# Projection weights squared and halved three tiles after their loads, sparse keys and queries loaded one tile ahead, in a hybrid attention step

## The chip, the cores and the metric

The kernel runs on one core of a Trainium2 chip. The core's engines work side by side, each through its own list of instructions in order: PE (TensorE, matrix products), DVE (VectorE), ACT (ScalarE), POOL (GpSimd), and SP (SyncE), which here only issues transfers. ACT and POOL can issue transfers too; a transfer is then an entry in that engine's list. An instruction waits at the head of its engine until what it reads has been written and what it overwrites has been read, and all that stands behind it on the engine waits with it. The metric is the time of one execution on the device in microseconds (us).

## The reference

One step of a layer with two kinds of attention on a prompt of 1024 tokens and on 8 sequences of 8 new tokens (the samples), each with 512 cached ones. The width is 1024, a head has 64 columns.

```python
h = rms_norm(x, g_norm)
proj = einsum('btd,dn->btn', h, w_in)      # w_in: 1024 x 3872, split into q, k, v, gates of both kinds
# NSA: 8 query heads, 2 key/value heads; compressed blocks, selected blocks, a window of 512
o_a = g0 * attend(q, kc, vc) + g1 * attend(q, k_selected, v_selected) + g2 * attend(q, k_window, v_window)
# FoX: 8 heads, softmax(q k / 8 + sum of log forget gates), causal
o_b = fox(q, k, v, cumsum(log f))
y = x + concat(o_a * silu(z_a), o_b * silu(z_b)) @ w_out
```

Keys and queries are normalised per head (QK-norm), those of NSA turned by rotary angles. The outputs are y for prompt and samples and the new keys and values of every cache.

## The kernel before

**The projection in chunks.** The columns of w_in are worked off in 15 chunks, of 256 columns each but one of 288: cmp, slc, win, qa twice, kb twice, qb twice, vb twice, z four times. For each chunk there are nine tiles: eight of 128 prompt tokens and one of the 64 sample tokens. PE cannot take the wide floats at full rate, so x and the weights are each halved into a high and a low part of 16 bits. A prompt tile is 24 products (eight slices of the width, three products each, the line of `acc<-wsp,xth` and `acc<-wsp,xtl`, L246); a sample tile is 16 (`acc<-wsp,xts`, L239). The weights change from chunk to chunk, so all nine tiles of a chunk read the chunk's halves, wsp.

**Loading and halving weights.** `load_w` gets a chunk's weights ready in four quarters: quarter q is loaded into a buffer wst (L198, on SP, four buffers in all), squared on ACT with a running sum by row (vsq, L202, the sums in the columns of vst). A product with ones on PE (tr, L205) adds the rows up; DVE (L206, L207) and POOL (a power, L208) make a scale of it. Then each quarter is scaled and split: ACT writes the high half (L216 and L217, or L220 alone), DVE (L221) or POOL (L218) the low one, both into wsp, of which there are eight, for two chunks. Called at tile 1 of a chunk, `load_w` is written for the next chunk. The first product of the next chunk cannot start before its first quarter is split.

**Background.** While the chunks run, other work is traced in between at tile 3 of a chunk: the compression of cached keys (cpair is loaded, turned on PE into ctr at L467, copied by ACT into cx or cy at L469 and multiplied, sa, L475), masks, gates, and `wout_squares`, which loads two slices of w_out each time (xin) and squares them on ACT (xsq, L813) for the scale of w_out.

**What sets the order.** The program is traced in one order; a scheduler then orders each engine's list with a simulation of its own, in which a transfer takes a time that need not be the chip's. It moves an instruction ahead when that simulation has it ready. `tc.keep_in_program_order` holds an instruction behind the one that was traced just before it on its engine.

**FoX and the start of NSA.** After eleven chunks FoX attention runs, with the z chunks as filler: PE makes scores st, ACT exponentials pf (L716) and their high half phi (L719), PE multiplies with the values (pv). Near its end `nsa_first` starts the sparse attention, then `nsa_tile` runs eight tiles of 128 queries. For a tile t, `nsa_keys(t)` loads the tile's selected and window keys (kn, two transfers, L1056 and L1057) and `nsa_queries(t)` the queries (nq, L1069), from outputs and from scratch in DRAM. `split16` scales them on ACT in place (L1049), rounds to the high half (L1050) and subtracts on POOL. PE turns them, ACT copies them (k1a, nq) and issues a transfer within the core to the masked operands kma (L1065) and nqm (L1081). `nsa_tile(t)` calls both for tile t + 1 at its start. PE's scores for the maximum (smax, L1103) read kma and nqm.

Of the kernel before, what the change touches and what calls it, by code (L numbers as in the profile page):

```python
# [21 lines left out]
D = 1024  # L22
NT = 8
# [70 lines left out]
def layer_kernel(ctx, tc, a, o):  # L94
# [84 lines left out]
    bank = {"tr": ("ctr", 1), "acc": ("acc", 4, 288), "ws": 2}  # L179
    w_in = a["w_in"][0].rearrange("(kt p) n -> p kt n", p=128)  # L180

    def load_w(cols, vcols=None, vi=None, split=None):

        n = sum(c1 - c0 for c0, c1 in cols)
        sv = W.tile([128, 24], F32, name="vst", bufs=3)
# [8 lines left out]
        for q in range(4):  # L194
            s = W.tile([128, 2, 288], F32, name="wst", bufs=4)
            i = 0
            for c0, c1 in cols:
                nc.sync.dma_start(s[:, :, i:i + c1 - c0], w_in[:, 2 * q:2 * q + 2, c0:c1])  # L198
                i += c1 - c0
            sq = W.tile([128, 2, 288], F16, name="vsq", bufs=1)  # L200
            for c, x in spans:
                nc.scalar.activation(sq[:, :, c], s[:, :, c], AF.Square, accum_out=sv[:, x + q:x + q + 1])  # L202
            st.append(s)
        p = PS.tile([128, 12], F32, name="tr", bufs=bank["ws"])
        nc.tensor.matmul(p[:, 0:used], ones, sv[:, 0:used], start=True, stop=True)  # L205
        nc.vector.tensor_reduce(out=sv[:, 12:13], in_=p[:, 0:used], axis=AX.X, op=ALU.add)  # L206
# [20 lines left out]
        if vcols is not None:  # L227
# [3 lines left out]
            nc.gpsimd.tensor_tensor(vsc[:, vi, 0:1], sv[:, 17:18], nhalf[:, 0:1], op=ALU.pow)  # L231
            nc.vector.reciprocal(vsc[:, vi, 1:2], vsc[:, vi, 0:1])
            nc.vector.tensor_tensor(un[:, 3:4], vsc[:, vi, 0:1], un[:, 0:1], op=ALU.mult)
        return parts, n, un

    def sample_product(ps, x, w):
        for k in range(KT):
# [566 lines left out]

    w_out = a["w_out"][0].rearrange("(kt p) n -> p kt n", p=128)

    def wout_squares(ks):

        for k in ks:
            s = B.tile([128, D], F32, name="xin", bufs=5)  # L810
            tc.keep_in_program_order(nc.sync.dma_start(s, w_out[:, k]))
            junk = B.tile([128, D], F32, name="xsq")
            nc.scalar.activation(junk, s, AF.Square, accum_out=wsc[:, k:k + 1])  # L813

    def wout_scale():

# [9 lines left out]
    def wout_split(pool, k):  # L826
# [4 lines left out]
        for h in range(2):  # L831
# [11 lines left out]
    chunks += [("z", [(1304, 1560)], 0), ("z", [(1560, 1816)], 1), ("z", [(3360, 3616)], 2), ("z", [(3616, 3872)], 3)]  # L843
    tabs = {"cmp": None, "slc": 1, "win": 2, "qa": 0}
    background = {1: [cmp_weights, cmp_prompt_tokens], 2: [lambda: cmp_cached(0)], 3: [lambda: cmp_cached(1)],
                  4: [lambda: cmp_cached(2)], 5: [lambda: cmp_cached(3), lambda: wout_squares((0, 1))],
                  6: [sample_compressed, lambda: score_scales(), lambda: wout_squares((2, 3))],
                  7: [setup_masks, finish_gates, lambda: wout_squares((4, 5))],
                  8: [fox_decay, load_logf, lambda: wout_squares((6, 7))], 9: [fox_first, wout_scale]}

    def score_scales():

# [24 lines left out]
    def load_chunk(ci):  # L877
        kind, cols, c = chunks[ci]
        vi = {"slc": 0, "win": 1, "vb": 2 + c}.get(kind)
        return load_w(cols, None if vi is None else slice(128, 256) if vi < 2 else slice(0, 256), vi,  # L880
                      True if kind == "z" else None)

    def project_chunk(ci, tab, wn):
        kind, cols, c = chunks[ci]
# [64 lines left out]
    first_loads()  # L949
    x_tile(0)  # L950
    setup()
    loaded = load_chunk(0)
    x_tile(1)
    nc.sync.dma_start(rope, a["c_rope"])
    for ci in range(11):
        if ci == 9:
            vb16 = C.tile([128, NT, 8, 130], F16, name="vb16", tag="vb16")
            nc.vector.memset(vb16[:, :, :, 64:65], 1.0)
        w = loaded
        for t in project_chunk(ci, tab, w):  # L960
            if t == 1:
                loaded = load_chunk(ci + 1)
            if t == 3:
                for f in background.get(ci, ()):
                    f()
    S1.close()


# [13 lines left out]
    def rest():  # L982
        w = loaded
        for ci in range(11, 15):
            n = None
            for t in project_chunk(ci, tab, w):
                if t == 1 and ci < 14:
                    n = load_chunk(ci + 1)
                yield t
            w = n  # L990

    filler = rest()
    quota = [0.0]
# [54 lines left out]
    def split16(src, s, hi, lo, e=nc.gpsimd):  # L1048
        nc.scalar.activation(src, src, AF.Copy, scale=s)  # L1049
        nc.scalar.activation(hi, src, AF.Copy)  # L1050
        e.tensor_sub(lo, src, hi)

    def nsa_keys(t):
        ks = BN.tile([128, 4, 128], F16, name="nks", bufs=1)
        kn = BN.tile([128, 4, 64], F32, name="kn")
        nc.sync.dma_start(flat(kn[:, 0:2]), outs["slc"][0][t * 128:(t + 1) * 128, 0:128])  # L1056
        nc.sync.dma_start(flat(kn[:, 2:4]), p_win[(t - 4) * 128:(t - 3) * 128, 0:128] if t >= 4 else kpark[t])  # L1057
        split16(kn, nsc[:, 0:1], ks[:, :, 0:64], ks[:, :, 64:128], nc.gpsimd if t else nc.vector)
        p = turned(t)
        for i in range(4):  # L1060
            nc.tensor.transpose(p[:, i * 128:(i + 1) * 128], ks[:, i], ident16)
        pk = p.rearrange("p (i n) -> p i n", i=4)
        c = slice(t * 128, (t + 1) * 128)
        nc.scalar.activation(k1a[:, :, c], pk, AF.Copy)
        nc.scalar.dma_start(kma[0:64, :, c], k1a[0:64, :, c])  # L1065

    def nsa_queries(t):
        q = BN.tile([128, 8, 64], F32, name="nq", bufs=1)
        nc.sync.dma_start(q.rearrange("p h d -> p (h d)"), qpark[t])  # L1069
        qsp = BN.tile([128, 8, 128], F16, name="nqs", bufs=1)  # L1070
        split16(q, nsc[:, 1:2], qsp[:, :, 64:128], qsp[:, :, 0:64], nc.gpsimd if t else nc.vector)
        r = []
        for g in range(2):
            p = turned(t)
            for i in range(4):
                nc.tensor.transpose(p[:, i * 128:(i + 1) * 128], qsp[:, 4 * g + i], ident16)
            q1 = BN.tile([128, 512], F16, name="nq1", bufs=4)
            qm = BN.tile([128, 512], F16, name="nqm", bufs=4)
            nc.gpsimd.memset(qm[64:88], 0.0)
            nc.scalar.activation(q1, p, AF.Copy)  # L1080
            nc.scalar.dma_start(qm[0:64], q1[64:128])  # L1081
            r.append((q1, qm))
        return r
# [104 lines left out]

    def nsa_first():

        nc.gpsimd.memset(kmc, 0.0)
        nc.gpsimd.memset(k1c, 0.0)
        nc.gpsimd.dma_start(kma[64:88].rearrange("p k n -> p (k n)"), a["c_kind"][:, 0:4 * T])
        for g in range(2):
            nc.gpsimd.dma_start(kmc[64:88, g, 64 * g:64 * g + 64], a["c_kind"][:, 4 * T:4 * T + 64])
        nc.gpsimd.dma_start(stair, a["c_stair"])
        nsa_keys(0)
        qq = nsa_queries(0)
        csp = BN.tile([64, 2, 128], F16, name="csp", bufs=1)
        nc.vector.memset(csp, 0.0)  # L1200
        split16(ck_p, nsc[0:63, 0:1], csp[0:63, :, 0:64], csp[0:63, :, 64:128])
        p = turned(0)
        for g in range(2):
# [220 lines left out]
    units = [(b, f, g) for b in range(NB) for f, g in ((sample_nsa, sample_nsa_out), (sample_fox, sample_fox_out))]  # L1424
    units.append((None, None, None))

    def nsa_tile(t, qq):
        qn = None
        if t + 1 < NT:
            nsa_keys(t + 1)  # L1430
            qn = nsa_queries(t + 1)
        oa = B3.tile([128, 8, 64], F32, name="oa", bufs=6)
        if t:
            nsa_max(1, t, qq[1][1])
# [22 lines left out]
    fox_early(7)  # L1457
    for g in range(2):
        nsa_max(g, 0, qq[g][1])
    fox_attend(7, 1)  # L1460
    SC.close()
    BE = B3 = S3.enter_context(tc.tile_pool(name="nsl", bufs=1, reuse_waits="tile"))
# [14 lines left out]
    mixed[0] = 1  # L1477
    for t in range(4):
        load_wout(2 * t)
        qq = nsa_tile(t, qq)  # L1480
    for _ in filler:
        pass
    rate = 0
# [171 lines left out]
```

## Time and profile before

| what | us |
|---|---|
| median of three runs | 971.22 (966.18 to 974.58) |
| the profiled execution | 971.47 |
| its span, first to last instruction | 969.7 |
| PE busy in it | 901.2 |
| DVE busy | 652.5 |
| ACT busy | 642.3 |
| POOL busy | 368.0 |
| mean granted clock of PE | 0.979 of full speed |

The profile counts an engine as busy while it works on an instruction, not while it waits or issues transfers. What is left of the span on PE, 68.5 us, is idle; 14.3 us of it lie in the first 20 us, before the first weights are there. Where the granted clock is below 1, PE is busy for longer with the same work; it has two levels here, 2.4 GHz (1.0) and 1.2 GHz (0.5), and a mean between them is a mix. In a timeline the bracket at the end of a row gives the time that the engine sat idle just before it, and what it waited for.

### The profile page before, as it was taken

The page shows a single profiled execution, that of the slowest core. Times are in us where ns is not written, and L with a number is a line of the kernel's source. Part 1 is how long each engine was busy: PE and PEld are TensorE (multiplying, and loading weights), DVE is VectorE, ACT ScalarE, POOL GpSimd, SP SyncE. Part 2 cuts the span into 40 slices and gives each one's busy share as a digit, 9 for nine tenths or more (in the row PEclk, how much of TensorE's full clock was granted, in tenths as well). Part 3 has the DMA queues.
Part 4 walks back from the last instruction along what each step waited for, and adds up shares of the span by engine and source line. Part 5 has one row for each costly group of instructions (what it writes and reads, how often), then busy time and mean ns, then how long its engine had stood idle before and what let it go on. Part 6 is the DMA issues. An engine that isn't in the chain of part 4 may idle for free. (4 is left out here: it accounts for less than half of the span.)

```text
span 969.7 us, 24710 instructions
## 1 busy us (share of the span) xinstructions
PE 901.2 (93%) x9099; PEld 679.7 (70%) x9099; DVE 652.5 (67%) x1894; ACT 642.3 (66%) x1379; POOL 368.0 (38%) x548
## 2 busy tenths in 40 slices
PE   4899999999999999999999888889999989999997
PEld 3688799788887888877777566566666656555554
DVE  5764665564555425687887666797978796778755
ACT  6754643443456554987886688887988966557662
POOL 4535657755677441361522311343321312101211
PEclk9899999999999999999999799999999999999999
DMA  7563324332345342354452755755455323213221
GB/s 267 141 151 110 85 67 116 99 98 82 94 142 198 97 115 84 91 164 151 152 169 70 221 166 157 231 161 183 153 172 196 91 66 99 96 56 88 92 94 66
DMA packets 125756, 124.32 MB, mean 128 GB/s; under 512 B 39404, under 2 KB 103572, under 8 KB 125612
## 3 DMA queue, kind: packets, MB, share of 16 engines
q1 hardware_dynamic: 120900, 119.07, 40.2%
q10 hardware_dynamic: 4048, 2.43, 1.0%
q0 software_dynamic: 688, 1.25, 0.6%
q8 instruction: 71, 1.16, 0.5%
q14 instruction: 49, 0.40, 0.1%
HBM read 87.96 MB, written 31.61 MB: 123 GB/s over the span
## 5 line engine op out<-in xcount | busy, mean ns | idle before, releaser
L246 PE MATMUL acc<-wsp,xth 128*128 128x256 f16 (+1 forms) x1920 | 337.4, 277 | 5.7 <-ACT xth L176 2.8
L246 PE MATMUL acc<-wsp,xtl 128*128 128x256 f16 (+1 forms) x960 | 265.4, 277 | 0.0
L246 PEld LDWEIGHTS <-xth 128*128 128x128 f16 x1920 | 188.5, 99 | 35.5 <-issue 3.3
L1152 ACT ACTIVATE pf<-st,nsc 128x512 f32<-128x512 f32 x132 | 98.7, 780 | 22.4 <-PE st L1148 13.1
L246 PEld LDWEIGHTS <-xtl 128*128 128x128 f16 x960 | 95.1, 99 | 14.8 <-issue 1.4
L729 PEld LDWEIGHTS <-phi 128*128 128x128 f16 x816 | 77.4, 97 | 15.2 <-ACT phi L719 3.3
L731 PEld LDWEIGHTS <-plo 128*128 128x128 f16 x816 | 77.2, 100 | 9.5 <-DVE plo L1155 2.6
L1153 ACT ACTIVATE phi<-pf 128x1024 f16<-128x1024 f32 (+1 forms) x76 | 71.3, 948 | 18.5 <-PE pv L731 15.1
L730 PEld LDWEIGHTS <-phi 128*128 128x128 f16 x816 | 77.2, 98 | 5.7 <-issue 0.6
L1155 DVE TENSOR_TENSOR plo<-pf,phi 128x1024 f16<-128x1024 f32 (+1 forms) x58 | 64.8, 1123 | 13.8 <-ACT phi L1153 13.3
L265 POOL TENSOR_TENSOR nss<-nss,nhalf 128x4 f32<-128x4 f32 (+3 forms) x72 | 68.8, 956 | 4.4
L716 ACT ACTIVATE pf<-st,nsc 128x512 f32<-128x512 f32 (+1 forms) x96 | 63.0, 673 | 9.4 <-PE st L782 4.7
L1155 POOL TENSOR_TENSOR plo<-pf,phi 128x1024 f16<-128x1024 f32 (+1 forms) x18 | 36.7, 2040 | 78.7 <-ACT phi L1153 66.5
L202 ACT ACTIVATE vsq<-wst 128x512 f16<-128x512 f32 (+2 forms) x72 | 40.1, 558 | 31.5 <-DMA wst<-in_w_in_dram 31.1
L729 PE MATMUL pv<-va,phi 128*128 128x65 f16 x528 | 58.5, 193 | 2.6 <-DVE nt L1132 1.7
L730 PE MATMUL pv<-va,phi 128*128 128x64 f16 x528 | 58.3, 195 | 0.0
L731 PE MATMUL pv<-va,plo 128*128 128x65 f16 x528 | 56.1, 192 | 1.6 <-DVE plo L1155 1.1
L1103 PE MATMUL smax<-kma,nqm 88*128 88x512 f16 (+3 forms) x192 | 49.9, 317 | 4.4 <-DMA nqm<-nq 2.0
L1147 PE MATMUL st<-nqm,kma 88*128 88x512 f16 x132 | 50.3, 381 | 2.3 <-ACT pf L1152 1.9
L719 ACT ACTIVATE phi<-pf 128x512 f16<-128x512 f32 (+1 forms) x96 | 48.8, 526 | 5.3 <-PE pv L731 5.0
L721 DVE TENSOR_TENSOR plo<-pf,phi 128x512 f16<-128x512 f32 (+3 forms) x77 | 46.9, 617 | 7.0 <-ACT phi L719 4.8
L749 DVE CUSTOM_DVE_ANT_0 junk<-smax,maskw,nm 128x512 bf16<-128x512 f32 x64 | 47.6, 743 | 4.4 <-PE smax L1103 2.9
(465 smaller groups left out, 2351.1 us busy)
## 6 DMA issues: line engine op xcount, KB each, us to landing
wst<-in_w_in_dram SPq DMA_DIRECT2D x56, 256.0 KB
sfk<-in_cache_fox_kv_dram SPq DMA_DIRECT2D x32, 256.0 KB
sfv<-in_cache_fox_kv_dram SPq DMA_DIRECT2D x32, 256.0 KB
out_dram<-kv SPq DMA_DIRECT2D x52, 128.0 KB
xin<-in_x_prompt_dram SPq DMA_DIRECT2D x8, 512.0 KB
cpair<-in_cache_nsa_cmp_kv_dram SPq DMA_DIRECT2D x64, 64.0 KB
xin<-in_w_out_dram SPq DMA_DIRECT2D x8, 512.0 KB
zpark<-z SPq DMA_DIRECT2D x32, 128.0 KB
```

The source lines that it names most:

```text
L246: nc.tensor.matmul(ps[:, :n], x[:, k, t * 128:(t + 1) * 128], w[k // 2][:, i, k % 2, :n], start=(k == 0 and j == 0), stop=(k == KT - 1 and ...
L265: nc.gpsimd.tensor_tensor(ss[:n, 0, :h], ss[:n, 1, :h], nhalf[:n, :h], op=ALU.pow)
L716: nc.scalar.activation(p[:n, :cols], ps[:n, :cols], AF.Exp, bias=nsc[:n, 3:4], scale=nsc[:n, 6:7])
L719: nc.scalar.activation(hi[:n, :cols], p[:n, :cols], AF.Copy)
L729: nc.tensor.matmul(po[:, s, 0:65], hi[:, c], v[:, 0:65], start=f, stop=False, skip_group_check=True)
L730: nc.tensor.matmul(po[:, s, 0:64], hi[:, c], v[:, 65:129], start=False, stop=False, skip_group_check=True)
L731: nc.tensor.matmul(po[:, s, 0:65], lo[:, c], v[:, 0:65], start=False, stop=l, skip_group_check=True)
L1103: nc.tensor.matmul(pr[:, r], qm[0:88, (r0 + r) * 128:(r0 + r + 1) * 128], kma[0:88, 2 * k + g, j0 * 128:j1 * 128], start=r == 0, stop=not ...
L1147: nc.tensor.matmul(ps, kma[0:88, 2 * k + g, c], qm[0:88], start=True, stop=False)
L1152: nc.scalar.activation(pf[:, 512 * x:512 * x + 512], ps, AF.Exp, bias=nsc[:, 3:4], scale=nsc[:, 2:3])
L1153: nc.scalar.activation(hi[:, 0:n], pf[:, 0:n], AF.Copy)
L1155: (nc.gpsimd if turn[0] % share[mixed[0]] == 0 else nc.vector).tensor_sub(lo_[:, 0:n], pf[:, 0:n], hi[:, 0:n])
```

## The change

`load_w` becomes a generator with two stops. At tile 1 of a chunk it issues the loads of the next chunk's weights; at tile 4 it goes on with squares, sum, scale and halving. From chunk 1 on its squares are held in program order. `wout_squares` likewise issues two loads at one call and squares them at the next, held in order. For the sparse attention a new function `nsa_load(t)` issues the three loads of a tile's keys and queries from ACT's queue instead of SP's, a tile ahead of `nsa_keys(t)` and `nsa_queries(t)`; the queries get a second buffer. Keys and queries of tile 1 are traced before the last FoX head group instead of after it.

```diff
-    def load_w(cols, vcols=None, vi=None, split=None):
+    def load_w(cols, vcols=None, vi=None, split=None, pin=False):
...
+            st.append(s)
+        yield
+        for q in range(4):
             sq = W.tile([128, 2, 288], F16, name="vsq", bufs=1)
             for c, x in spans:
-                nc.scalar.activation(sq[:, :, c], s[:, :, c], AF.Square, accum_out=sv[:, x + q:x + q + 1])
-            st.append(s)
+                i = nc.scalar.activation(sq[:, :, c], st[q][:, :, c], AF.Square, accum_out=sv[:, x + q:x + q + 1])
+                if pin:
+                    tc.keep_in_program_order(i)
...
-        return parts, n, un
+        yield parts, n, un
...
-    def wout_squares(ks):
+    wo = []
+    def wout_squares(*ks):
+        while wo:
+            k, s = wo.pop(0)
+            junk = B.tile([128, D], F32, name="xsq")
+            tc.keep_in_program_order(nc.scalar.activation(junk, s, AF.Square, accum_out=wsc[:, k:k + 1]))
         for k in ks:
             s = B.tile([128, D], F32, name="xin", bufs=5)
             tc.keep_in_program_order(nc.sync.dma_start(s, w_out[:, k]))
-            junk = B.tile([128, D], F32, name="xsq")
-            nc.scalar.activation(junk, s, AF.Square, accum_out=wsc[:, k:k + 1])
+            wo.append((k, s))
...
+    def next_chunk(ci, t, g):
+        if t == 1:
+            g.append(load_chunk(ci + 1))
+            next(g[0])
+        elif t == 4:
+            g[0] = next(g[0])
...
+    def nsa_load(t):
+        kn = BN.tile([128, 4, 64], F32, name="kn")
+        nc.scalar.dma_start(flat(kn[:, 0:2]), outs["slc"][0][t * 128:(t + 1) * 128, 0:128])
+        nc.scalar.dma_start(flat(kn[:, 2:4]), p_win[(t - 4) * 128:(t - 3) * 128, 0:128] if t >= 4 else kpark[t])
+        q = BN.tile([128, 8, 64], F32, name="nq", bufs=2)
+        nc.scalar.dma_start(q.rearrange("p h d -> p (h d)"), qpark[t])
+        ahead[t] = kn, q
...
+    def nsa_next(t):
+        nsa_keys(t)
         if t + 1 < NT:
-            nsa_keys(t + 1)
-            qn = nsa_queries(t + 1)
+            nsa_load(t + 1)
+        return nsa_queries(t)
...
     for g in range(2):
         nsa_max(g, 0, qq[g][1])
+    qn = nsa_next(1)
     fox_attend(7, 1)
```

In the changed file the lines are a few numbers on: L202 is L206 there, L205 is L210, L216 to L221 are L221 to L226, L239 is L244, L246 is L251, L813 is L819, L1049 is L1069, and the loads L1056, L1057 and L1069 are L1077, L1078 and L1080.

PE, at the sum of the squares of the second qb chunk's weights. Before, it stands in the third prompt tile of the first qb chunk:

```order
L592 MATMUL ctr<-ident,coc 64x64 x2
L246 LDWEIGHTS xth
L246 MATMUL acc<-wsp,xth 128x256
L246 LDWEIGHTS xth
L246 MATMUL acc<-wsp,xth 128x256
L246 LDWEIGHTS xtl
L246 MATMUL acc<-wsp,xtl 128x256
L205 MATMUL tr<-vst,ones 128x4
L246 LDWEIGHTS xth
L246 MATMUL acc<-wsp,xth 128x256
```

Now it stands behind the eight prompt tiles of that chunk; lc and ones are FoX's sums of log gates:

```order
L251 MATMUL acc<-wsp,xtl 128x256
L643 MATMUL ctr<-lc,tri 128x64
L645 MATMUL ctr<-lc,ones 128x56
...
L645 MATMUL ctr<-lc,ones 128x16
L210 MATMUL tr<-vst,ones 128x4
L244 LDWEIGHTS xts
L244 MATMUL acc<-wsp,xts 128x256
...
L645 MATMUL ctr<-lc,ones 128x8
L251 LDWEIGHTS xth
L251 MATMUL acc<-wsp,xth 128x256
```

The sum has moved from the third prompt tile to behind the eighth; only the 16 sample products and one small product stand between it and the first product that reads the new halves.

ACT, at the start of the sparse attention (csp and nks are rounded halves, k, q, ksp and qsp FoX's operands, zt the gate path). Before:

```order
L719 ACTIVATE phi<-pf 128x512
L716 ACTIVATE pf<-st,nsc 128x512
L1049 ACTIVATE kn<-kn,nsc 128x256
L716 ACTIVATE pf<-st,nsc 128x384
L705 ACTIVATE q_5832<-tr 128x512
L671 ACTIVATE qsp<-kql 128x4x64
L407 ACTIVATE zt<-ssum,un 64x256
L1049 ACTIVATE nq<-nq,nsc 128x512
```

And now, from the transfer of the second tile's window keys on:

```order
L1078 DMA kn<-kpark 128x128
L706 ACTIVATE k_5831<-tr 128x512
L1080 DMA nq<-qpark 128x512
L1069 ACTIVATE kn<-kn,nsc 128x256
L1069 ACTIVATE nq<-nq,nsc 128x512
L1070 ACTIVATE csp<-ck_p 63x2x64
L1069 ACTIVATE kn<-kn,nsc 128x256
```

The loads are entries of ACT's list now, and the second scaling of kn, which is the second tile's, stands five rows behind the load that it reads. For the third tile:

```order
L1077 DMA kn<-out_dram 128x128
L1078 DMA kn<-kpark 128x128
L1080 DMA nq<-qpark 128x512
L721 ACTIVATE pf<-st,nsc 128x384
L724 ACTIVATE phi<-pf 128x512 x2
L1069 ACTIVATE kn<-kn,nsc 128x256
```

Three exponential and rounding steps and the load of the queries stand between the load of the keys and their scaling.

## Rows read from the trace of the kernel before

**Rows 1.** The page, first part: engines' busy time, share, instructions.
```profile
PE 901.2 (93%) x9099; PEld 679.7 (70%) x9099; DVE 652.5 (67%) x1894; ACT 642.3 (66%) x1379; POOL 368.0 (38%) x548
```

**Rows 2.** Stretches: from:to, us; busy of PE, PEld, DVE, ACT, POOL; clock, DMA, GB/s.
```profile
35.00:45.00 10.00, 6.96 (x35) 5.05 (x34) 6.89 (x15) 8.64 (x20) 5.62 (x10) 0.66 0.61 145
188.20:191.60 3.40, 3.40 (x19) 2.40 (x17) 2.38 (x9) 1.05 (x3) 2.40 (x4) 0.50 0.37 97
300.00:312.00 12.00, 9.92 (x77) 8.24 (x76) 7.42 (x37) 8.07 (x21) 9.81 (x16) 0.86 0.44 135
540.00:553.00 13.00, 12.38 (x84) 7.21 (x83) 9.23 (x27) 10.62 (x25) 1.65 (x2) 0.50 0.75 205
597.00:601.00 4.00, 3.41 (x24) 2.82 (x25) 1.28 (x2) 1.77 (x5) 0.25 (x1) 0.60 0.51 132
```

**Rows 3.** Waits of ACT: us in total, times, longest.
```profile
ACT vsq L202 <- DMA wst<-in_w_in_dram: 31.1, 29, 4.0
...
ACT xsq L813 <- DMA xin<-in_w_out_dram: 6.3, 5, 3.3
```

**Rows 4.** Timeline of ACT, then PE, around 184 us: start, length, instruction.
```profile
184.38 0.63 ACT L202 ACTIVATE vsq<-wst 128x512 f16<-128x512 f32 x1 [4.00 <-DMA wst<-in_w_in_dram]
...
186.88 0.64 ACT L469 ACTIVATE cy<-ctr 128x256 f32<-128x256 f32 x2
...
187.57 0.66 PE L467 MATMUL ctr<-ident,cpair 128*128 128x128 f32 x4 [2.38 <-ACT cy L469]
```

**Rows 5.** PE's groups by line and form: busy, mean ns; idle before, releaser.
```profile
L246 PE MATMUL acc<-wsp,xth 128*128 128x256 f16 x1792 | 313.5, 276 | 5.7 <-ACT xth L176 2.8 <-DVE z L408 0.8 <-ACT wsp L220 0.8
...
L467 PE MATMUL ctr<-ident,cpair 128*128 128x128 f32 x80 | 12.4, 277 | 6.9 <-ACT cy L469 4.8 <-ACT cx L469 2.1
...
L205 PE MATMUL tr<-vst,ones 128*128 128x8 f32 x6 | 1.1, 250 | 2.1 <-ACT vsq L202 2.1
```

**Rows 6.** Timeline: three halvings, each from PE's sum to POOL's last half.
```profile
208.11 0.28 PE L205 MATMUL tr<-vst,ones 128*128 128x4 f32 x2
...
218.46 1.54 POOL L218 TENSOR_TENSOR wsp<-wst,wsp 128x512 f16<-128x512 f32 x1
...
244.66 0.28 PE L205 MATMUL tr<-vst,ones 128*128 128x4 f32 x2
...
252.12 1.16 POOL L218 TENSOR_TENSOR wsp<-wst,wsp 128x512 f16<-128x512 f32 x1
...
272.78 0.28 PE L205 MATMUL tr<-vst,ones 128*128 128x4 f32 x2
...
278.66 1.15 POOL L218 TENSOR_TENSOR wsp<-wst,wsp 128x512 f16<-128x512 f32 x1
```

**Rows 7.** Timeline of PE: products of a prompt tile, then the samples' 16.
```profile
181.86 0.38 PE L246 MATMUL acc<-wsp,xth 128*128 128x256 f16 x2
...
182.19 0.38 PE L246 MATMUL acc<-wsp,xth 128*128 128x256 f16 x2
...
196.80 1.91 PE L239 MATMUL acc<-wsp,xts 128*128 128x256 f16 x16
```

**Rows 8.** Timeline at the sparse start: SP's issue, ACT's scaling, PE's two gaps.
```profile
533.58 0.44 SPq L1057 DMA_DIRECT2D kn<-kpark  x1
...
538.34 0.51 ACT L1049 ACTIVATE kn<-kn,nsc 128x256 f32<-128x256 f32 x1 [2.31 <-DMA kn<-kpark]
...
539.46 0.22 PE L779 MATMUL st<-qm,km 104*128 104x128 f16 x1 [2.53 <-ACT pf L716]
...
597.59 0.47 PE L1103 MATMUL smax<-kma,nqm 88*128 88x256 f16 x2 [1.98 <-DMA nqm<-nq]
```

**Rows 9.** Timeline of ACT and its queue: a transfer issued by ACT, a copy.
```profile
609.27 0.69 ACTq L1065 DMA_DIRECT2D kma<-k1a  x1
609.44 0.31 ACT L1348 ACTIVATE ot<-ctr 64x64 f32<-64x64 f32 x2
```

**Rows 10.** The page's costliest groups: the rounding step of FoX.
```profile
L719 ACT ACTIVATE phi<-pf 128x512 f16<-128x512 f32 (+1 forms) x96 | 48.8, 526 | 5.3 <-PE pv L731 5.0
```

More of the change, by code (lines that the diff above doesn't have):

```diff
@@ L845, in layer_kernel @@
     background = {1: [cmp_weights, cmp_prompt_tokens], 2: [lambda: cmp_cached(0)], 3: [lambda: cmp_cached(1)],
[L846 to L849, printed above, removed]
+                  4: [lambda: cmp_cached(2)], 5: [lambda: cmp_cached(3), lambda: wout_squares(0, 1)],
+                  6: [sample_compressed, lambda: score_scales(), lambda: wout_squares(2, 3)],
+                  7: [setup_masks, finish_gates, lambda: wout_squares(4, 5)],
+                  8: [fox_decay, load_logf, lambda: wout_squares(6, 7)], 9: [fox_first, wout_squares, wout_scale]}
     def score_scales():
@@ L880, in load_chunk @@
         return load_w(cols, None if vi is None else slice(128, 256) if vi < 2 else slice(0, 256), vi,
-                      True if kind == "z" else None)
+                      True if kind == "z" else None, ci > 0)
+    def next_chunk(ci, t, g):
[4 more added lines that the diff above has]
+            g[0] = next(g[0])
     def project_chunk(ci, tab, wn):
@@ L951, in layer_kernel @@
     setup()
-    loaded = load_chunk(0)
+    for loaded in load_chunk(0):
+        pass
     x_tile(1)
@@ L959, in layer_kernel @@
         w = loaded
+        g = []
         for t in project_chunk(ci, tab, w):
-            if t == 1:
-                loaded = load_chunk(ci + 1)
+            next_chunk(ci, t, g)
             if t == 3:
@@ L965, in layer_kernel @@
                     f()
+        loaded = g[0]
     S1.close()
@@ L984, in rest @@
         for ci in range(11, 15):
-            n = None
+            g = []
             for t in project_chunk(ci, tab, w):
-                if t == 1 and ci < 14:
-                    n = load_chunk(ci + 1)
+                if ci < 14:
+                    next_chunk(ci, t, g)
                 yield t
-            w = n
+            w = g[0] if g else None
     filler = rest()
@@ L1051, in split16 @@
         e.tensor_sub(lo, src, hi)
+    ahead = {}
+    def nsa_load(t):
[5 more added lines that the diff above has]
+        ahead[t] = kn, q
     def nsa_keys(t):
         ks = BN.tile([128, 4, 128], F16, name="nks", bufs=1)
-        kn = BN.tile([128, 4, 64], F32, name="kn")
-        nc.sync.dma_start(flat(kn[:, 0:2]), outs["slc"][0][t * 128:(t + 1) * 128, 0:128])
-        nc.sync.dma_start(flat(kn[:, 2:4]), p_win[(t - 4) * 128:(t - 3) * 128, 0:128] if t >= 4 else kpark[t])
+        kn = ahead[t][0]
         split16(kn, nsc[:, 0:1], ks[:, :, 0:64], ks[:, :, 64:128], nc.gpsimd if t else nc.vector)
@@ L1067, in nsa_queries @@
     def nsa_queries(t):
-        q = BN.tile([128, 8, 64], F32, name="nq", bufs=1)
-        nc.sync.dma_start(q.rearrange("p h d -> p (h d)"), qpark[t])
+        q = ahead[t][1]
         qsp = BN.tile([128, 8, 128], F16, name="nqs", bufs=1)
@@ L1189, in nsa_first @@
     def nsa_first():
+        for t in range(2):
+            nsa_load(t)
         nc.gpsimd.memset(kmc, 0.0)
@@ L1425, in layer_kernel, with nsa_tile @@
     units.append((None, None, None))
-    def nsa_tile(t, qq):
-        qn = None
+    def nsa_next(t):
+        nsa_keys(t)
         if t + 1 < NT:
-            nsa_keys(t + 1)
-            qn = nsa_queries(t + 1)
+            nsa_load(t + 1)
+        return nsa_queries(t)
+    def nsa_tile(t, qq, qn=None):
+        if qn is None and t + 1 < NT:
+            qn = nsa_next(t + 1)
         oa = B3.tile([128, 8, 64], F32, name="oa", bufs=6)
@@ L1479, in layer_kernel @@
         load_wout(2 * t)
-        qq = nsa_tile(t, qq)
+        qq = nsa_tile(t, qq, None if t else qn)
     for _ in filler:
```

## The prediction

> **What bounds the kernel now.** I read the page first, then the waits, then the groups by line, then the timeline around the longest gaps. The first part of the page says that PE is busy 901.2 of 969.7 us, ACT 642.3 [rows 1]. So only what makes PE idle, or slows its clock, can be won back, and both are visible. The stretches show the clock: 188.2 to 191.6 us ran at a granted clock of 0.50, the 1.2 GHz level of the two, and 540 to 553 us the same, while PE had work all the time [rows 2]. Such a stretch costs half its length. It comes after a gap: PE had stood still for 2.38 us before the first and for 2.53 us before the second [rows 4, 8].
>
> The changed code meets PE's gaps in two stages.
>
> In the projection (20 to 308 us) ACT's waits are headed by the square of the raw weights, vsq, which waited 31.1 us in all for the load of wst [rows 3]. ACT works in order, so what stands behind a waiting square waits too: the square at 184.38 us had waited 4.00 us, behind it stood the evictions cy at 186.88, and PE, which needed cy's tile for its next transposes, was idle 2.38 us until 187.57 [rows 4]. The groups by line add up this sort: 6.9 us before the transposes of cpair (on cy and cx), 2.8 us before xth's product (ACT then waited for the halving's scale), 2.1 us before the column sum tr of the squares [rows 5]. That is 11.8 us. The clock adds 10 us at 0.66, 3.4 us at 0.50 and 12 us at 0.86 [rows 2]: 3.4 + 1.7 + 1.7 = 6.8 us. **Together 18.6 us of this stage can be tied to squares and halving.**
>
> At the start of the sparse attention (from 533 us) the scaling of kn at 538.34 waited 2.31 us for its load, and PE was idle 2.53 us [rows 8]; the slow stretch of 13 us behind it cost 6.5 us [rows 2]. Later PE waited 1.98 us for the masked queries nqm at 597.59 [rows 8], with 4 us at 0.60 behind it, 1.6 us [rows 2]. **Together 12.6 us.**
>
> **The change part by part, against this execution's own time, 971.5 us** (969.7 of span and 1.8 around it, 0.3 above the median of the runs, 971.2).
>
> *Loads ahead of squares.* Nothing is added or removed: the 72 squares and 56 loads of 256 KB stay. In the new order the loads stand about a chunk ahead of their squares, so the DMA waits should go, and with them the 18.6 us.
>
> *Halving behind squares.* This is moved, and it is where I expect the time to come back. Before, the column sum tr<-vst stood in tile 2 of the chunk before, six tiles of 24 products ahead of the first product that needs the halves; a tile takes 24 x 0.109 = 2.6 us (three products in 0.33 us [rows 7]), so some 16 us of PE work covered it. Now it stands near that chunk's end. From tr<-vst to the last low half (POOL's wsp) took, in the chunks of 256 columns before z, between 7.0 us (272.78 to 279.81) and 11.9 us (208.11 to 220.00), with 8.6 us in one between them (244.66 to 253.28) [rows 6]. I take 8.6: the longest had its first step late behind other DVE work, and such work drains while PE stands. The first tile of the next chunk reaches the last quarter of the weights after 18 products, 2.0 us, so PE stands still where the cover is under 6.6 us. The cover, counted in the new order of PE, is products of 0.109 us and the samples' 16 (1.75 us), with 0.3 for the sum itself [rows 7]; the three chunk ends with the compression's products in them have over 9 us:
> slc to win 31 products and the samples, 5.4 us, a stall of 1.2; win to qa 6.2, 0.4; kb to qb 7.2, none; first qb to second, only the samples, 2.1, a stall of 4.5; to vb 4.8, 1.8; between the vb 3.2, 3.4; vb to z 3.7, 2.9. Sum 14.2 us. Three are well over the 2.38 us that let the clock fall, and cost 1.7 us each as that one did: 5.1. **New cost 19.3 us, so this stage changes by +0.7 us.** With a chain of 7.0 us the same list gives 6.2 + 1.7 = 7.9 us (net -10.7); with 11.9 us, 36.7 + 7 x 1.7 = 48.6 us (net +30). Below no cost at all it cannot go, for the work is the same.
>
> *Squares of w_out a call later, pinned.* ACT's wait for xin, 6.3 us in five waits [rows 3], goes. No group of PE names it as the end of its idle time, so I cost it at nothing; its cover is PE's own queue of products. If it held evictions after all, it is worth up to 6.3 us. The squares now stand among the pinned ones of the next weights, which is in the chain above.
>
> *Sparse keys and queries.* 24 issues leave SP for ACT's queue, and the transfers behind them on SP may start sooner; nothing in the rows waits for those. An issue there held ACT's queue for 0.69 us at 609.27, and a copy on ACT started at 609.44 beside it [rows 9]; I cost the 24 at nothing, and at most 24 x 0.69 = 17 us if each stops ACT. The program issues the loads a tile ahead, but the scheduler has hoisted the scaling too. A load of kn took 4.8 us from issue to use (533.58 to 538.34) [rows 8]. With activations of about half a us (the scaling 0.51 [rows 8], phi 0.526 [rows 10]), the new rows of ACT leave, between issue and scaling, 2.6 us for the second tile's keys, 2.3 for the third's, some 3.3 and 2.8 for queries of the fourth and keys of the fifth, and nothing but the issue, 0.5, for the queries of the fifth. Waits: 2.2 + 2.5 + 1.5 + 2.0 + 4.3 = 12.5 us on ACT. PE followed ACT's 2.31 us with 2.53 here, but later tiles have the samples' work as filler, so I take three quarters, 9.4 us, and two slow stretches of 1.6 us: 12.6, which is just what is won. **Zero**, between -8.6 (4 us reach PE, no slow stretch) and +8 (all 12.5 us, and slow stretches of 6.5 and 1.6 as now).
>
> Sum: 971.5 + 0.7 + 0 = **972 us**.
>
> **What the Trainium skill would say.** DMA: Bandwidth & Descriptors, section Rules for kernel authors, advises to issue a DMA early, compute, and wait on its semaphore late, as the fixed cost then overlaps. The trace agrees on the half that it shows, the 31.1 us of waits right behind issues; that all of it becomes time is the third rival.
>
> **The rivals.**
> First, *the halving is quick and the loads land in time*: chain of 7.0 us, sparse start at its low end, 971.5 - 10.7 - 8.6 = 952 us. For it: with PE waiting, DVE, POOL and ACT have little else to do. Against: most chains measured were longer.
> Second, on the slow side, *the halving becomes the clock of the projection*. Its place are the four ends from the first qb to z. The chain competes there with evictions that the FoX work adds and with w_out's squares between the pinned ones. The point from which it decides is a chain of about 9.6 us, where every one of the four ends has over 2.5 us of stall and slows the clock; half way to its longest, with half of the sparse start's upper bound, it gives 971.5 + 15 + 4 = 990 us.
> Third, *every wait for these loads vanishes and none takes its place*: 971.5 - 18.6 - 12.6 = 940 us. For it stands only that loads now lead by a chunk. Against it stands the place of tr<-vst. That is what the rule of the Trainium skill named above amounts to here.
> That the second part does not do what it says (a load a tile ahead, but a scaling straight behind it) is in my forecast already.
>
> **How the numbers follow.** Chances: forecast 0.39, range of its own 963 to 981; first rival 0.26; second 0.28; third 0.07. About 1% (9.7 us) is what a measurement of this kernel can tell from no change. Faster by more than that are the first and third, less an edge of the first: 0.31. Slower is the second, less an edge: 0.27. The rest, 0.42, is within 1%. The range of 8 in 10 takes in most of the first rival and most of the second, 950 to 992, and leaves out the third and the far ends.
>
> **What would show each step right or wrong.** In the profile after: waits of vsq for wst near zero (if still over 10 us, the loads do not lead). PE idle with xth's product released by ACT's or POOL's wsp at the ends of chunks, about 4.5 us at the first qb's; if there is none over 2 us, the halving is covered and the time is near 950. Scaling of kn and nq on ACT still waiting for DMA, 12 us in all; if under 4, the sparse start has won. The stretches after 536 us at 0.50 for 13 us or not. Wrong would be the whole account if the projection's end moved by over 10 us without any such row.

## The result: 1.2% slower

The changed kernel takes 982.71 us (976.62 to 987.07, four runs) against 969.89 us (966.18 to 974.58, four runs) before: ratio 1.0116, 95% interval 1.0076 to 1.0156. The forecast was 972 with 950 to 992. The profiled execution after is the quickest of its four, 976.62 us; the others have a lower granted clock (0.972 to 0.977 against 0.980). So the trace shows 5 of the some 12 us. Lost to the clock (span times what the mean clock lacks to 1) are 23.8 us in the mean of these four runs, and 17.5 in the mean of 15 runs of the kernel before (two slower ones left out); the rest of the time is 958.5 and 953.8 us. By this measure somewhat over half of the loss is clock. It is an upper bound for the clock: it counts slow stretches in which PE was waiting anyway.

The page after, first part, answers to [rows 1]: PE has the same products and the same busy time.

```profile
PE 901.3 (92%) x9099; PEld 677.2 (69%) x9099; DVE 643.3 (66%) x1894; ACT 644.1 (66%) x1379; POOL 367.6 (38%) x548
```

What differs is where PE stands. Here are the stages as stretches, cut at the same products: the first ends with the samples' 16 products of the first vb chunk, the second with those of the last z chunk, the rest by 100 us. The columns are those of [rows 2]. Before:

```profile
20.00:346.00 326.00, 311.27 (x2733) 271.31 (x2732) 185.64 (x664) 169.80 (x468) 192.53 (x313) 0.98 0.41 117
346.00:533.00 187.00, 180.21 (x2000) 148.37 (x1999) 130.25 (x356) 142.02 (x302) 63.18 (x76) 1.00 0.41 124
533.00:600.00 67.00, 58.01 (x631) 39.58 (x628) 42.25 (x119) 53.54 (x124) 15.67 (x26) 0.86 0.65 194
600.00:700.00 100.00, 92.50 (x1116) 62.51 (x1115) 82.03 (x249) 85.02 (x173) 35.00 (x45) 0.99 0.58 179
...
900.00:969.00 69.00, 63.25 (x575) 35.42 (x573) 40.73 (x84) 37.79 (x55) 9.65 (x16) 1.00 0.25 85
```

After:

```profile
20.00:335.00 315.00, 305.34 (x2729) 269.07 (x2728) 186.83 (x658) 162.72 (x454) 187.86 (x309) 0.99 0.41 117
335.00:526.00 191.00, 181.58 (x1981) 148.41 (x1979) 127.22 (x353) 145.22 (x312) 64.68 (x81) 0.98 0.41 126
526.00:600.00 74.00, 64.51 (x731) 43.31 (x730) 47.26 (x137) 61.62 (x142) 18.50 (x29) 0.91 0.66 194
600.00:700.00 100.00, 89.12 (x1069) 60.53 (x1066) 73.11 (x242) 82.43 (x167) 32.25 (x43) 0.97 0.63 193
...
900.00:974.00 74.00, 64.49 (x598) 35.48 (x594) 44.79 (x96) 40.64 (x59) 12.07 (x15) 0.95 0.19 68
```

Length less PE's busy time is idle. The first stage is 11 us shorter (idle 14.7, now 9.7; clock 0.98, now 0.99). The second is 4 us longer (idle 6.8, now 9.4; clock 1.00, now 0.98). From there to the end of the span it takes 436.7 us before and 448.9 after, 12.2 more: -11 + 4 + 12.2 is the 5.2 us between the two spans. Part of the last figure is PE's work that has moved there from the stages ahead, some 20 products by the counts; the idle time in it is 3.4 us more from 600 to 700 us and 3.8 more in the last stretch.

**What the change was meant to do, it did.** ACT's waits for DMA after, in total, times, longest, answer to [rows 3]:

```profile
ACT pf L721 <- DMA kn<-kpark: 3.8, 1, 3.8
...
ACT nq L1069 <- DMA nq<-qpark: 3.1, 2, 2.4
...
ACT vsq L206 <- DMA wst<-in_w_in_dram: 2.4, 1, 2.4
...
ACT xsq L819 <- DMA xin<-in_w_out_dram: 1.6, 2, 0.9
...
ACT kn L1069 <- DMA kn<-out_dram: 1.1, 2, 0.7
```

The squares' 31.1 us are 2.4, those of w_out 1.6 for 6.3. PE's groups by form after, columns of [rows 5]:

```profile
L251 PE MATMUL acc<-wsp,xth 128*128 128x256 f16 x1792 | 313.0, 275 | 10.7 <-POOL wsp L223 3.9 <-ACT wsp L225 2.5 <-ACT wsp L222 1.9
...
L472 PE MATMUL ctr<-ident,cpair 128*128 128x128 f32 x80 | 12.0, 273 | 0.0
...
L210 PE MATMUL tr<-vst,ones 128*128 128x8 f32 x6 | 0.9, 228 | 0.0
```

The idle time before the transposes of cpair (6.9 us) and before the sum tr (2.1) is gone; that before the products with xth has doubled, from 5.7 to 10.7, and its releasers are now the three engines that write the halves (wsp). The last group that changed is at the other end of the program, the transposes of the last tile's z, before and then after:

```profile
L1589 PE MATMUL ctr<-ident,z 128*128 128x128 f32 x8 | 1.6, 283 | 0.7 <-ACT z L1516 0.7
```

```profile
L1623 PE MATMUL ctr<-ident,z 128*128 128x128 f32 x8 | 1.9, 323 | 4.8 <-ACT z L1550 4.8
```

**Three theories** came out of this: *late halving* (squares and halving at tile 4 leave too little work before the next chunk), *the exposed end* (nothing left for PE while the last tile is normalised), and *the sparse loads* (issued from ACT, in ACT's way). The rival to all of them is that any of the parts, by a new order, costs as much by chance.

### The profile page after: what moved, and what is told of

Read it like the earlier page. It is cut to its first block, busy times and chain, and to the rows that moved or that the text cites. A ratio compares the mean times of both kernels' runs of the same rounds, so it can differ in the third digit from the quotient of the medians.

```text
span 974.9 us, 24737 instructions
## 1 busy us (share of the span) xinstructions
PE 901.3 (92%) x9099; PEld 677.2 (69%) x9099; DVE 643.3 (66%) x1894; ACT 644.1 (66%) x1379; POOL 367.6 (38%) x548
## 3 DMA queue, kind: packets, MB, share of 16 engines
q0 software_dynamic: 688, 1.25, 0.7%
## 5 line engine op out<-in xcount | busy, mean ns | idle before, releaser
L251 PE MATMUL acc<-wsp,xth 128*128 128x256 f16 (+1 forms) x1920 | 336.9, 276 | 11.2 <-POOL wsp L223 4.4
L251 PE MATMUL acc<-wsp,xtl 128*128 128x256 f16 (+1 forms) x960 | 263.0, 275 | 0.0
L251 PEld LDWEIGHTS <-xth 128*128 128x128 f16 x1920 | 187.8, 99 | 35.5 <-issue 6.0
L251 PEld LDWEIGHTS <-xtl 128*128 128x128 f16 x960 | 94.7, 99 | 21.7 <-issue 8.1
L267 ACT ACTIVATE nsq<-acc 128x256 f32<-128x256 f32 (+1 forms) x64 | 22.4, 351 | 47.5 <-PE acc L251 47.5
```

The costliest lines, as they stand in the source:

```text
L251: nc.tensor.matmul(ps[:, :n], x[:, k, t * 128:(t + 1) * 128], w[k // 2][:, i, k % 2, :n], start=(k == 0 and j == 0), stop=(k == KT - 1 and ...
```

## The experiments

All ratios are to the kernel before, run beside them, with 95% intervals. Its medians in the three sets were 972.37, 972.55 and 970.0 us.

**Parts alone.** The weights and w_out without the sparse part:

```diff
-        nc.scalar.dma_start(flat(kn[:, 0:2]), outs["slc"][0][t * 128:(t + 1) * 128, 0:128])
+        nc.sync.dma_start(flat(kn[:, 0:2]), outs["slc"][0][t * 128:(t + 1) * 128, 0:128])
...
-    qn = nsa_next(1)
```

(the three loads stand in nsa_keys and nsa_queries again, as before)

> The change without its sparse part: keys and queries are loaded as before, on SP, behind their tile. Theory A (the projection part wins and keeps what it wins, the sparse part loses): the sample product of the second vb chunk starts about 8 us earlier than before, the whole is 960 to 965 us, ratio 0.990 to 0.996. Theory B (the late halving and the pins re-plan what follows, and the gain is given back in FoX and the sparse attention whatever the loads do): 968 to 980 us, ratio 0.998 to 1.010.

981.42 us, 1.0127 (1.0075 to 1.0178): theory B, above its range. The sparse part alone, on the kernel before:

> The sparse part alone: keys and queries loaded a tile ahead from ACT's queue, projection as before. Theory A: 980 to 990 us, ratio 1.010 to 1.020, with ACT idle 2 to 4 us behind an issue that itself waits near 540 us. Theory B: 965 to 973 us, ratio 0.995 to 1.003.

982.48 us, 1.0157 (1.0103 to 1.0210), in the range of theory A. The weights alone, with w_out's squares as before:

```diff
-            tc.keep_in_program_order(nc.scalar.activation(junk, s, AF.Square, accum_out=wsc[:, k:k + 1]))
...
+            junk = B.tile([128, D], F32, name="xsq")
+            nc.scalar.activation(junk, s, AF.Square, accum_out=wsc[:, k:k + 1])
```

> The weight loads and the halving of the change alone; squares of w_out and the sparse loads as before. If the squares of w_out matter as little as costed, within 3 us of the run without the sparse part. If ACT's 6.3 us of waits for w_out come back and hold evictions, 3 to 6 us above it.

989.62 us, 1.0212 (1.0157 to 1.0266), 8 us above the run without the sparse part and outside both expectations. And w_out's squares alone, on the kernel before:

> The squares of w_out a call after their loads, held in order, and nothing else of the change. Costed at nothing: ratio 0.997 to 1.003. If ACT's 6.3 us of waits for w_out held evictions: 0.993 to 0.997. If pinned squares hold back what is behind them on ACT: 1.003 to 1.008.

969.06 us, 0.9984 (0.9952 to 1.0016).

Each of the two larger parts costs by itself what both cost together, so a shared place is likely. But the two losses are not of one kind: by the split above, in the means of the runs, the weights and w_out lose 9.3 us at full clock and 1.5 of clock, the sparse part 3.9 and 8.9. PE's waits show one shared place: in the weights and w_out, and then in the sparse part alone, the last transposes wait as in the whole change.

```profile
PE acc L251 <- POOL wsp L223: 4.8, 6, 1.6
PE ctr L1609 <- ACT z L1536: 4.2, 2, 3.9
```

```profile
PE ctr L1603 <- ACT z L1530: 3.9, 1, 3.9
```

With w_out's squares alone this wait is 0.7 us, as before. The halving's waits (wsp) are 10 us with the weights and w_out, 7 with the weights alone, and 1.4 where the weights are not changed.

**The end of the program.** PE's last product with values (pv) ends at 961.31 us; then DVE finishes the attention, ACT and POOL normalise it, and PE waits. PE's timeline after: start, length, instruction, in brackets the idle time before it and its releaser.

```profile
961.12 0.19 PE L736 MATMUL pv<-va,plo 128*128 128x65 f16 x1
965.22 0.69 PE L1623 MATMUL ctr<-ident,z 128*128 128x128 f32 x2 [3.90 <-ACT z L1550]
966.38 0.61 PE L1631 MATMUL st<-woh,uh 128*128 128x512 f16 x1 [0.47 <-ACT uh L1624]
...
970.70 0.38 PE L1631 MATMUL st<-woh,ul 128*128 128x512 f16 x1
```

Before, PE did 12 products of the output projection, of tiles already there, in this gap, and waited 0.73 us:

```profile
957.93 0.19 PE L731 MATMUL pv<-va,plo 128*128 128x65 f16 x1
...
958.74 0.39 PE L1597 MATMUL ctr<-woh,uh 128*128 128x512 f16 x1 [0.48 <-ACT uh L1590]
...
961.12 0.38 PE L1597 MATMUL ctr<-woh,ul 128*128 128x512 f16 x1
962.24 0.44 PE L1589 MATMUL ctr<-ident,z 128*128 128x128 f32 x2 [0.73 <-ACT z L1516]
...
965.53 0.38 PE L1597 MATMUL st<-woh,ul 128*128 128x512 f16 x1
```

After, the new order has used them up earlier. In the gap the clock falls to its 1.2 GHz level (stretch after, columns of [rows 2]):

```profile
963.50:970.30 6.80, 4.61 (x12) 1.70 (x13) 1.03 (x4) 1.10 (x4) 0.74 (x2) 0.50 0.00 0
```

A product of 512 columns takes 0.61 us there against 0.39. From the end of the last pv to the end of PE's last product it takes 9.8 us (961.31 to 971.08), with 12 products of the output projection in it; before it took 7.8 us (958.12 to 965.91) with 24. Twelve of them take 2.6 us at full clock (958.74 to 961.12 are eleven), so the end costs 2.0 + 2.6 = 4.6 us more. The experiment holds 12 of those products behind the last pv, the first six in the bank of the pv tile, which is free by then:

```diff
-                ps = PS.tile([128, 512], F32, name="ctr", bufs=CTR) if early else PM.tile([128, 512], F32, name="st", bufs=2)
+                ps = (PM.tile([128, 512], F32, name="pv", bufs=PV) if ks.start == h == 0 else
+                      PS.tile([128, 512], F32, name="ctr", bufs=CTR) if early else PM.tile([128, 512], F32, name="st", bufs=2))
...
+                        if h == 1 and ks.start == k == j == 0:
+                            tc.keep_in_program_order(i)
```

> The whole change, and beside it twelve products of the last tile's output projection held behind the last product with the values (the first of them write into the buffer that this product frees, the others are pinned behind them), so that they run while DVE, ACT and POOL prepare the last quarter. Theory C (half of the loss is the end of the program, where the re-planned order has nothing left for PE): PE's gap of 3.9 us before the last transposes falls to under 1.5, and the time falls by 4 to 7 us against the change, to 976 to 979, ratio 1.004 to 1.008. Rival (the products only change places, and the end is set by ACT and DVE anyway): within 2 us of the change, ratio 1.010 to 1.014.

976.55 us, 1.0038 (1.0008 to 1.0068): two thirds of the loss are gone. PE's last pv ends at 963.98 here, it starts its held products at 964.92, and it has the transposes' values without a wait:

```profile
964.92 0.49 PE L1632 MATMUL pv<-woh,uh 128*128 128x512 f16 x1 [0.94 <-DVE nt L1159]
...
965.63 0.63 PE L1632 MATMUL pv<-woh,ul 128*128 128x512 f16 x1
...
969.21 0.38 PE L1623 MATMUL ctr<-ident,z 128*128 128x128 f32 x2
```

From the last pv to PE's end it is 8.9 us with 24 products, 3.5 us less than the change needs for as many; the rest of the 6 us between the medians doesn't stand in these rows. The clock falls here too, though PE stood for only 0.94 us: from 964.9 to 968.3 us it is 0.53, and most of the held products take 0.63 us each. The hold shortens the slow stretch from 6.8 to 3.4 us and doesn't remove it, so the long gap is not shown to be what lets the clock fall.

The same edit on the kernel before, and on the sparse part alone:

> The kernel before with the same edit at the end. Its own order already leaves twelve of these products behind the last product with the values. Theory C: no change, ratio 0.997 to 1.003. If the edit does something of its own, above all to the clock, 0.990 to 0.996.

972.31 us, 1.0007 (0.9979 to 1.0035): nothing, as its end was covered already.

> The sparse part alone with the end of the program held. It lost 1.6% without that, and its end had the same gap of 3.9 us as the change. If the end was 6 us of it, 976 to 979, ratio 1.005 to 1.009, and what is left is the sparse part's own cost; if the end matters less here, 980 to 984.

978.53 us, 1.0098 (1.0062 to 1.0134), where it was 1.0157 with the end exposed (the intervals overlap). From the last pv to PE's end the hold saves 2.6 us here (9.1 us both times, with 12 products more). The other 1.0% that the sparse part costs alone has no cause here; 5.5 of the 8 us between the means are clock by the measure above.

**The halving.** At tile 2 instead of tile 4; the loads stay at tile 1:

```diff
-        elif t == 4:
+        elif t == 2:
```

> The change with squares and halving one tile after the loads instead of three. The squares wait for loads again if the lead of the loads comes from the three tiles; if it comes from the loads standing ahead of the halving of the chunk before, they do not. If the halving at chunk ends is the cost in the projection: PE's 7 to 8 us of waits for wsp and hth there fall under 4, and the second vb chunk's sample product starts 3 to 5 us earlier than in the change; the whole 976 to 980. If the halving is not the cost: 981 to 985.

964.48 us, 0.9898 (0.9857 to 0.9939): 2.2% under the change, more than was expected, and faster than before. Its waits of PE for the halves are down to the first two of the program, and its squares still don't wait (PE's wait is first, ACT's second):

```profile
PE acc L251 <- ACT wsp L225: 0.8, 1, 0.8
...
PE acc L251 <- DVE wsp L226: 0.6, 1, 0.6
```

```profile
ACT vsq L206 <- DMA wst<-in_w_in_dram: 1.4, 1, 1.4
```

The samples' products of the last z chunk begin at 511.2 us, where they begin at 523.6 with the halving at tile 4 and at 529.8 before. Both edits together:

> The change with the halving one tile after the loads, and the end of the program held as in the run that pinned twelve products there. If the two add up (1.8% and 0.8% against the change): 955 to 960 us, ratio 0.982 to 0.987. If the end is covered by the earlier work already: 962 to 966.

962.40 us, 0.9914 (0.9885 to 0.9944). With the end held the halving's place is worth 1.2% (0.9914 against 1.0038). The hold itself shows no difference beside the early halving: 0.9914 and 0.9898 lie within each other's intervals, though the end of that kernel is exposed too (its last transposes wait 4.8 us). By the rows from the last pv to PE's end the hold saves 4.1 us there as well (10.4 us with 12 products, 8.8 with 24), about the width of these intervals. These two are the fastest kernels here.

**The sparse part.** The 24 loads issued from SP, in the whole change:

```diff
-        nc.scalar.dma_start(
+        nc.sync.dma_start(
```

> The whole change, but the 24 loads of keys and queries are issued from SP instead of ACT, still a tile ahead. Theory A in the form that ACT's queue is the cost (an issue that waits holds back ACT's exponentials): 962 to 970 us, no wait of 3.8 us of ACT near 536 us. If the loads a tile ahead and the earlier tile 1 are the cost, whatever the queue: 978 to 986 us. Theory B: 978 to 986 us as well.

977.99 us, 1.0060 (1.0032 to 1.0089): 0.6% under the change, and far from the 962 to 970 us that ACT's queue as the cost would have given. The same in the best version:

> The same with the sparse loads a tile ahead, but issued from SP. If it is ACT's queue that costs: 3 to 6 us below the run that issues them from ACT, as it was 4 below the change. If that difference was the draw of the order: within 2 us.

965.53 us, 0.9955 (0.9929 to 0.9980): 0.4% over it. And the best version without the sparse part:

> The same without the sparse part: keys and queries loaded on SP behind their tile, as before. If the sparse part of the change costs time of its own (ACT's issues that wait, more of the slow clock): 3 to 8 us below the run with it, 948 to 956. If it is worth what it was meant to be: 3 to 8 us above it. If the order of the sparse stage is all that differs: within 3 us.

966.80 us, 0.9966 (0.9937 to 0.9996), so beside the early halving and the held end the sparse part gains 0.5%, with intervals that overlap; alone, with the end held, it cost 1.0%.

What ACT's queue does to ACT is plain in the change, at the start of the sparse stage. ACT's timeline after (ACTq is its queue of issues), then PE's:

```profile
535.09 0.34 ACTq L1077 DMA_DIRECT2D kn<-out_dram  x1
535.38 0.76 ACT L721 ACTIVATE pf<-st,nsc 128x512 f32<-128x512 f32 x1
538.05 0.33 ACTq L1078 DMA_DIRECT2D kn<-kpark  x1
539.53 0.33 ACTq L1080 DMA_DIRECT2D nq<-qpark  x1
539.96 0.67 ACT L721 ACTIVATE pf<-st,nsc 128x384 f32<-128x384 f32 x1 [3.81 <-DMA kn<-kpark]
```

```profile
540.68 0.26 PE L784 MATMUL st<-qm,km 104*128 104x128 f16 x1 [1.73 <-ACT pf L721]
```

The three issues of one tile, one behind the other in the program, are spread over 4.4 us. ACT does no arithmetic between 536.14 and 539.96, and the instruction that follows has nothing to do with these loads. With the loads on SP neither kernel has such a row (pf or phi behind kn); nor has the one with the halving at tile 2 alone, whose loads are on ACT. But the time moved one way in the one and the other way in the other, each time by so little that the intervals still touch. That this wait costs the kernel anything isn't shown.

**Before and behind the last z chunk, over the kernels.** One cut runs through these traces: the start of the samples' products of the last z chunk, and what is left from there to the end of the span (us).

| kernels | the products start at | from there to the end |
|---|---|---|
| before; with the end held; with w_out's squares alone | 529.8, 531.1, 528.0 | 439.9, 439.4, 439.8 |
| sparse part alone; with the end held | 525.9, 526.5 | 451.0, 447.3 |
| halving at tile 4: the change; with the end held; loads from SP; weights and w_out; weights alone | 523.6, 527.7, 525.9, 523.2, 525.0 | 451.3, 448.9, 452.1, 456.2, 465.5 |
| halving at tile 2; with the end held; with loads from SP too | 511.2, 507.0, 508.1 | 458.1, 455.1, 451.4 |

The first two rows halve the weights as before and still differ by 5 us, so a few us in one trace are no finding. The early halving stands clear of that: about 19 us sooner. The late one is 3 us sooner in the mean and not slower. And every kernel with the weights or the sparse part changed needs 7 to 26 us more behind this cut, the fastest ones too. Of the change's 11.4 us the end is 4.6; what orders the rest so wasn't found.

## Why the prediction was right, and where it was not

The likeliest case was no change, at 972 us with 963 to 981 of its own; the measured 982.7 lies just above that, inside the range, on the way to the second rival at 990. The sum came near by errors that cancelled: in front of the last z chunk the change gains 3 us in the mean of the traces (6 in the two profiled executions compared above) where +0.7 was forecast, and behind it loses 11 where nothing was. That the time lies in the range is luck in good part.

**Loads ahead of squares: right.** The 18.6 us tied to squares and halving were there to win: with the halving at tile 2 the last z chunk comes that much sooner. ACT's waits fell as said, the transposes of cpair wait no more. The first stage is 11 us shorter, after the new stalls at its chunk ends. One term of the 18.6 was none: the 3.4 us for the stretch of 10 us at 0.66 [rows 2]. In the sparse part alone, where the squares are as before, the same stretch has as many products (36 for 35) at full clock, with more idle time instead:

```profile
35.00:45.00 10.00, 4.62 (x36) 3.37 (x37) 7.78 (x18) 9.78 (x27) 5.75 (x12) 1.00 0.64 149
```

PE was waiting there anyway, and a slow clock only filled the wait. The third rival fell: 29 us less waiting for loads on ACT did not make the kernel faster until the halving was put back as well. What the Trainium skill (DMA: Bandwidth & Descriptors, Rules for kernel authors) says, that a load issued early and waited for late overlaps its fixed cost, the trace bears out for the waits, 2.4 us where there were 31.1; the time did not follow.

**Halving behind squares: the chain was right, the cover was not.** 8.6 us was taken from the sum to the last low half. At the four ends from the first qb on it took 9.2 (280.69 to 289.88), 9.0, 9.5 and 9.9 us, to POOL's last half; at the first of them DVE's last one came 0.7 us later still. Forecast stalls of 4.5, 1.8, 3.4 and 2.9 us, 12.6 together, measured 2.2, 0.6, 2.4 and 2.5, 7.6 together. Another 1.52 us of PE's idle time at the first end stands behind FoX's nch on DVE. PE's rows at these ends:

```profile
284.69 0.38 PE L251 MATMUL acc<-wsp,xth 128*128 128x256 f16 x2 [1.75 <-ACT wsp L225]
285.48 0.27 PE L251 MATMUL acc<-wsp,xth 128*128 128x256 f16 x1 [0.41 <-DVE wsp L226]
...
289.99 0.39 PE L657 MATMUL ctr<-ident,nch 128*24 128x128 f16 x4 [1.52 <-DVE nch L651]
...
313.05 0.27 PE L251 MATMUL acc<-wsp,xth 128*128 128x256 f16 x1 [0.59 <-POOL wsp L223]
...
335.93 0.27 PE L251 MATMUL acc<-wsp,xth 128*128 128x256 f16 x1 [0.37 <-DVE wsp L226]
...
337.60 0.60 PE L251 MATMUL acc<-wsp,xth 128*128 128x256 f16 x4 [0.42 <-ACT wsp L222]
...
340.32 0.27 PE L251 MATMUL acc<-wsp,xth 128*128 128x256 f16 x1 [1.57 <-POOL wsp L223]
...
362.70 0.27 PE L251 MATMUL acc<-wsp,xth 128*128 128x256 f16 x1 [1.50 <-ACT wsp L222]
...
363.94 0.27 PE L251 MATMUL acc<-wsp,xth 128*128 128x256 f16 x1 [0.97 <-POOL wsp L223]
```

The step that failed is "the first tile of the next chunk reaches the last quarter of the weights after 18 products". POOL's first low half at the first of these ends began here:

```profile
287.62 2.26 POOL L223 TENSOR_TENSOR wsp<-wst,wsp 128x512 f16<-128x512 f32 x2
```

Two halves share this row, so the first was done at about 288.7 us. From 284.69 to then PE ran 28 products, more than the 24 of a whole tile, and no tile can be finished without POOL's halves: PE was taking the first quarters of further tiles into the other three accumulators (`acc` has four). So this stall is set by when the first quarter comes, not the last; at the third end 1.57 of 2.4 us still go to a half of POOL's. No wait was as long as the 2.38 us after which the clock fell before, and no slow stretch followed at these ends. One did come later, at 441 us, where the halving for z met the FoX work; the 3.3 us before it held 1.25 us of idle time in gaps of at most 0.69:

```profile
441.30:448.10 6.80, 5.63 (x25) 3.46 (x24) 5.38 (x10) 6.74 (x13) 4.45 (x4) 0.50 0.93 296
```

That the late place of the halving costs, the second rival's mechanism, is shown by moving it: 1.2 to 2.2% for two tiles. But against the kernel before it did not become the clock of the projection, as that rival has it: the last z chunk's samples come 6 us sooner in the profiled run (523.6 for 529.8; 3 us in the mean of the traces), a small part of it by products moved behind. With the halving at tile 2 they come 19 us sooner. That is what was left lying, and some 8 us of it reach the end of the kernel.

**Squares of w_out at nothing: right alone** (0.9984). Beside the late squares of the weights it is worth 0.8% (1.0127 against 1.0212), with intervals that overlap a little.

**Sparse start at zero: right at its place, by another balance.** Waits for these loads come to 8.0 us on ACT (3.1 and 1.1 in the scaling, 3.8 in pf) where 12.5 was expected. From the last z to 600 us PE is idle 9.5 us (9.0 before), and the slow stretch has stayed:

```profile
533.40:547.10 13.70, 10.20 (x98) 7.25 (x97) 6.85 (x18) 8.94 (x19) 1.47 (x2) 0.50 0.87 236
```

What failed is "24 issues at nothing": one group of three kept ACT from its next work for 3.8 us, and PE stood 1.7 of it, though what that costs in the end isn't shown.

**Left out altogether: the end of the program.** No step looked behind 601 us. The end, 4.6 us in the profiled run by its rows and 0.8% by the experiment, is the largest single piece of the loss that was found. No load stands in its waits, and it appears with the weights alone and with the sparse part alone: what differs is the order in which the scheduler, given other instructions upstream, spends the products that could fill the last gap.

**What stays open.** More than half of what the change loses behind the last z chunk, and all but the end of what the early halving gives back there, has no cause here. From 600 to 700 us there are 3.4 us more idle time after the change and about as much in the best version (cut by time, not at the same products); nothing was tried on it. Why SP's queue seems to help in one order and to hurt in the other isn't known, nor what the spread-out issues waited for. Of the 6.3 us more that the clock costs in the mean run, the trace of the quickest run shows none; in the kernels with held ends and the early halving it is less (20.1 us lost with the end held, 15.8 with both), but where it falls in the longer runs was not seen.

## What to carry to other kernels

Moving a load ahead of its use is only safe if the work that consumes it stays where it had cover: split the two, issue early, but leave the computation about where it was (tile 2 here, not tile 4). When a change makes a scheduler order everything anew, read the last 15 us of the program first: what PE has left for the final chain of small steps is decided far upstream, and it can be held there. And when two parts each cost what both cost together, look for a shared place, but check that it accounts for both: holding the end gave back two thirds of the change's loss and less than half of the sparse part's.

## What the hardware showed that was not expected

A transfer issued from a compute engine's queue is not free for that engine when the issue has to wait: ACT stood 3.81 us behind three issues of 0.33 us each. TensorE's clock fell to its lower level for 6.8 us at 441 us, behind gaps of at most 0.69 us, but stayed up at 284 us, where PE stood 1.75, 0.41 and then 1.52 us:

```profile
284.00:290.00 6.00, 3.38 (x29) 2.64 (x28) 5.44 (x15) 4.81 (x10) 3.54 (x6) 1.00 0.28 78
```

Before, 3.4 and 13 us of it had followed gaps of 2.38 and 2.53 us. After, the 13.7 us at 533.4 began behind gaps of at most 0.38 us, ahead of the 1.73 us that PE then stood; and behind a gap of 0.94 us at the held end it fell in the change with its end held (0.63 us a product) and stayed up in the best version with loads from SP (0.38, after 0.93 us). The size of a single gap did not tell which. And four runs of the changed kernel lost between 19.5 and 27.6 us to the clock, a spread of 8 us, two thirds of the difference that was to be explained.
